# 204 unread single-pass products, in place of twelve unread two-pass ones, in TensorE's first wait of a four-layer trunk

## The chip, the cores and the metric

The kernel runs on one NeuronCore of a Trainium2 chip. The metric is the device time of one execution in microseconds (us); of several runs the median is given. Five engines share the core: TensorE (PE, with its weight loads listed apart as PEld), VectorE (DVE), ScalarE (ACT), GpSimd (POOL) and SyncE (SP, which here only issues transfers). Each runs its own list of instructions in order, and they wait for one another by semaphores.

## The reference

512 rows of 1024 numbers pass through four layers. Each layer normalises the rows, adds a mixer, normalises again and adds a gated feed-forward block. The mixers are, in order, a diagonal state-space mixer (s5), a gated linear attention, a differential attention, and the s5 mixer again. Only the beginning of the first s5 layer matters here. Its core, cut down:

```python
dt = exp(log_dt);  ab_mag = exp(lr * dt);  ab_ang = li * dt
ab_re = ab_mag * cos(ab_ang);  ab_im = ab_mag * sin(ab_ang)
bb = f * b                                   # complex, f from ab and lam
s[t] = ab * s[t-1] + bb @ u[t]               # a scan over the 512 rows
y[t] = real(c @ s[t]) + d_skip * u[t]
z = gelu(y);  a, b = split(z @ w_glu);  x = x + a * sigmoid(b)
```

## The kernel before, in words

Everything is float32. Large products are done as three single-pass products (`mm3`, lines 432 to 434): each operand is split into a high and a low part of type float32r, and high by high, high by low and low by high are summed in one PSUM bank. A single-pass product is one record in the trace. A product of two plain float32 operands, such as a transpose through the identity, takes two passes and leaves two records. Every product has a held operand of 128 rows by up to 128 columns, which a weight load puts into the array, and a streamed operand of up to 512 columns.

`run` calls the layers one after the other, and `s5_first` (line 1594 on) is the first of them. It allocates `zT`, a tile of 128 partitions by 8192 float32r numbers, which the pipeline fills much later (line 1488, from about 56 us on) with the transposed outputs of the mixer. Then it does the following, in the order of the program:

- `s5_small` loads the parameters and turns them with three small transposes (L920, L935). DVE then computes exponentials, sines and powers from them in a long row of small instructions.
- SP queues the loads of `x`, the gains, and the matrices `b` and `c` of the state space (`s5_loads`: `bb` at L1105, `craw` at L1108).
- POOL clears parts of several tiles (`zero_off`, L1176 and L1177).
- `self.hand(PE, Activation)` (line 1639): from here TensorE and ScalarE execute in the order in which the program names the instructions. DVE, POOL and SP are still ordered by the framework's scheduler, until the pipeline calls `hand_all` and writes out the order for all five.
- `s5_qt` (L1141) turns `craw` on TensorE, which needs its transfer. Behind it `warmed(12)` issues twelve products of the identity with itself (L1193) into a bank that nobody reads.
- `s5_in` on ACT squares and scales `x` (L1382, L1383, L1375; POOL takes the root at L523). In between, `rows(0)` turns the phases' rows on TensorE (L1038) and copies them on ACT (L1039).
- DVE copies the turned `craw` into `Q` (L1160) and multiplies it with powers (L1095 to L1097).
- The pipeline `s5_pipe` works through eight groups `kk`. For the first ones, TensorE computes phases (`rough` L1055 and L1056, `angle` L1063 to L1065), turns the input (`up`, L1415) and the operators (`xps`, L1237), and forms the products `V` (L1436). ACT copies and takes sines (L1057, L1059, L1428, L1260, L1071 to L1073), DVE clips (L1068), modulates (L1441 to L1446) and scans (L1450). The map for the direct path goes from TensorE (L1203) over DVE (L1213), ACT (L1217) and two transfers through DRAM (L1219, L1228) to the products `y` (L1470, L1472).

In the feed-forward blocks most products have 256 streamed columns (L575), in the projections 512 (L432 to L434).

Of the kernel before, what the change touches and what calls it, by code (L numbers as in the profile page):

```python
# [11 lines left out]
F32 = mybir.dt.float32  # L12
# [9 lines left out]
P = 128  # L22
# [302 lines left out]
class Trunk:  # L325
# [860 lines left out]
            else:  # L1186
                self.dq.dma_start(d[r, :, g], src[r])

    def warmed(self, n):

        ps = self.sbank("warmed")
        for _ in range(n):
            self.nc.tensor.matmul(ps[:, :P], self.ident[:], self.ident[:], start=True, stop=True)  # L1193

    def s5_rows(self, nb, bp, Q):

# [397 lines left out]
    def s5_first(self, ctx):  # L1594
        nc, i = self.nc, self.i
        xin = self.xp.tile([P, NT, D], F32, tag="x", name="xin")
        zpool = ctx.enter_context(self.tc.tile_pool(name="zT0", bufs=1, side="right"))
        zT = zpool.tile([P, 2, KT, SEQ], F32R, name="zT")
        self.edge(zpool, 32)
        with self.tc.tile_pool(name="s5_0", bufs=1) as p:  # L1600
            scr, more = (self.hp.tile([P, 4096], F32, tag="hT", name=f"scr{z}") for z in range(2))
            oms = [more[:, 1024 * z : 1024 * z + 1024].rearrange("p (a b) -> p a b", a=2) for z in range(2)]
# [33 lines left out]
            with self.tc.issue_after(self.last_power.ins):  # L1636
                new_x(0)
                X[0][2]()
            self.hand(mybir.EngineType.PE, mybir.EngineType.Activation)
            with self.tc.issue_after(self.last_sine.ins):  # L1640
                ps = self.s5_qt(raw[0][1])
                self.warmed(12)
                hu = self.s5_in(scr, xin, (rounded, rows[0]))
            with self.tc.issue_after(self.last_row.ins):
                X[0][3]()
# [6 lines left out]
            room = [four[:, n] for n in range(4)] + [wide[:, 512:], self.np_.tile([P, 512], F32, tag="R", name="z1", bufs=1)[:]]  # L1652
# [851 lines left out]
```

## Time and profile before

| | |
|---|---|
| median of 3 runs | 2279.58 us (2279.41 to 2284.47) |
| span of the profiled execution, first to last instruction | 2272.3 us |
| the profiled execution's own time | not recorded apart from its span; the median lies 7.3 us above it |
| PE busy | 2198.1 us (97%) |
| DVE busy | 1584.4 us (70%) |
| ACT busy | 1109.9 us (49%) |
| POOL busy | 328.0 us (14%) |
| granted TensorE clock, mean | 0.996 |

The span is what the trace shows of one execution; what lies around it (start and end of the program) is in the median alone. A busy share says how long an engine had something to do, not that it set the pace: PE is the bound of most of the span, but in its first 46 us it waits often, and the pace is then set by what it waits for. In rows of the timeline the columns are start (us), length (us), engine, line, operation, output and inputs, shape, count, and in brackets the idle time before and what ended it. Several equal instructions in a row are merged into one line with their count; the length then runs from the first start to the last end.

### The profile page before, as it was taken

How to read it: one execution, taken by the hardware profiler on the slowest of the kernel's cores; microseconds unless marked ns; L12 is line 12 of the kernel's file. 1: busy time of each engine (PE TensorE's matmuls, PEld its weight loads, DVE VectorE, ACT ScalarE, POOL GpSimd, SP SyncE). 2: the span in 40 equal slices, each digit the busy share in tenths (PEclk: the TensorE clock that was granted, in tenths of full speed). 3: DMA queues.
4: the chain of work that ended last, by engine and by line, in shares of the span. 5: the costliest groups of instructions: out<-in, count | busy, mean ns of one | idle time of the engine just before them, and what ended most of it. 6: DMA issues, size and time to landing. Idle time of an engine off the chain costs nothing. (4 is left out here: it accounts for less than half of the span.)

```text
span 2272.3 us, 37257 instructions
## 1 busy us (share of the span) xinstructions
PE 2198.1 (97%) x14871; PEld 1955.4 (86%) x14871; DVE 1584.4 (70%) x2413; ACT 1109.9 (49%) x1779; POOL 328.0 (14%) x446
## 2 busy tenths in 40 slices
PE   6999999999999999999999999999999899999998
PEld 5888889889777799998988887999999888989997
DVE  9965878786525488777745676976766965957675
ACT  6634545454443355554435675644534224635343
POOL 6401142421000010100002231110000000101000
PEclk9999999999999999999999999999999999999999
DMA  4356666663322556665247465985641555766622
GB/s 88 64 171 167 166 157 179 163 180 93 114 76 66 153 154 177 181 172 154 94 139 149 98 148 135 230 213 143 170 100 57 141 155 147 194 172 157 168 75 75
DMA packets 294504, 319.92 MB, mean 141 GB/s; under 512 B 70141, under 2 KB 233241, under 8 KB 294202
## 3 DMA queue, kind: packets, MB, share of 16 engines
q1 hardware_dynamic: 231706, 235.79, 34.1%
q0 software_dynamic: 62624, 81.75, 19.4%
q8 instruction: 117, 1.92, 0.3%
q14 instruction: 57, 0.47, 0.1%
HBM read 285.62 MB, written 16.65 MB: 133 GB/s over the span
## 5 line engine op out<-in xcount | busy, mean ns | idle before, releaser
L412 DVE TENSOR_TENSOR whl<-wst,whl 128x1024 fp32r<-128x1024 f32 x272 | 331.9, 1225 | 267.7 <-ACT whl L404 267.0
L404 ACT CAST whl<-wst 128x1024 fp32r<-128x1024 f32 x272 | 284.5, 1051 | 342.5 <-PE acc L434 242.2
L575 PE MATMUL a<-side,whl 128*128 128x256 f32 x3168 | 383.0, 277 | 6.7 <-DVE whl L412 6.0
L575 PEld LDWEIGHTS a<-side,whl 128*128 128x128 f32 x3168 | 370.2, 188 | 8.9 <-DVE whl L412 6.8
L432 PE MATMUL acc<-whl,act 128*128 128x512 f32 x704 | 278.9, 396 | 1.8 <-DVE g L620 1.6
L433 PE MATMUL acc<-whl,act 128*128 128x512 f32 x704 | 275.7, 392 | 0.0
L434 PE MATMUL acc<-whl,act 128*128 128x512 f32 x704 | 275.7, 392 | 0.0
L575 PE MATMUL c<-side,whl 128*128 128x256 f32 x2112 | 254.8, 277 | 3.6 <-DVE whl L412 3.6
L575 PEld LDWEIGHTS c<-side,whl 128*128 128x128 f32 x2112 | 246.6, 188 | 4.5 <-DVE whl L412 4.4
L412 DVE TENSOR_TENSOR whl<-slot,whl 128x1024 fp32r<-128x1024 f32 x105 | 127.9, 1222 | 64.2 <-ACT whl L404 64.1
L432 PEld LDWEIGHTS acc<-whl,act 128*128 128x128 f32 x704 | 132.6, 188 | 31.7 <-DVE g L620 2.0
L434 PEld LDWEIGHTS acc<-whl,act 128*128 128x128 f32 x704 | 132.5, 188 | 27.9
L433 PEld LDWEIGHTS acc<-whl,act 128*128 128x128 f32 x704 | 132.7, 189 | 26.2 <-issue 0.2
L404 ACT CAST whl<-slot 128x1024 fp32r<-128x1024 f32 x105 | 109.9, 1051 | 74.1 <-PE acc L434 28.2
L432 PE MATMUL acc<-whl,hT 128*128 128x512 f32 x352 | 142.1, 404 | 1.5 <-DVE ro L2233 1.5
L434 PE MATMUL acc<-whl,hT 128*128 128x512 f32 x352 | 137.6, 391 | 0.0
L433 PE MATMUL acc<-whl,hT 128*128 128x512 f32 x352 | 137.4, 390 | 0.0
L575 PE MATMUL d<-sides,whl 128*128 128x256 f32 x1056 | 133.6, 283 | 2.6 <-ACT whl L404 2.6
L575 PEld LDWEIGHTS d<-sides,whl 128*128 128x128 f32 x1056 | 128.9, 191 | 3.4 <-ACT whl L404 3.4
L575 PE MATMUL a<-sides,whl 128*128 128x256 f32 x1056 | 128.9, 278 | 1.7 <-DVE whl L412 1.2
L575 PEld LDWEIGHTS a<-sides,whl 128*128 128x128 f32 x1056 | 124.6, 188 | 3.0 <-DVE whl L412 1.4
L611 POOL DMA_DIRECT2D wst<-in_ffn_w_gate_up_dram x44 | 57.1, 1297 | 442.8 <-DMA wst<-in_ffn_w_gate_up_dram 159.6
(458 smaller groups left out, 3930.0 us busy)
## 6 DMA issues: line engine op xcount, KB each, us to landing
wst<-in_ffn_w_gate_up_dram SPq DMA_DIRECT2D x88, 512.0 KB, 4.4
wst<-in_ffn_w_down_dram SPq DMA_DIRECT2D x88, 512.0 KB, 4.4
slot<-in_ffn_w_gate_up_dram SPq DMA_DIRECT2D x69, 512.0 KB, 6.1
wst<-in_ffn_w_gate_up_dram POOLq DMA_DIRECT2D x44, 512.0 KB, 6.0
halves<-in_ffn_w_gate_up_dram SPq DMA_DIRECT2D x42, 512.0 KB, 5.6
wst<-in_s_w_glu_dram SPq DMA_DIRECT2D x32, 512.0 KB, 4.9
wst<-in_gla_w_in_dram SPq DMA_DIRECT2D x24, 512.0 KB, 3.6
wst<-in_diff_w_qkv_dram SPq DMA_DIRECT2D x24, 512.0 KB, 3.7
```

What stands on the lines that cost most here:

```text
L404: self.last["high"] = self.nc.scalar.copy(hl[:, 0], w[:])
L412: self.last["low"] = self.nc.vector.tensor_tensor(hl[:, 1], w[:], hl[:, 0].bitcast(F32), op=ALU.subtract)
L432: mm(out, lh, rh, start=first, stop=False)
L433: mm(out, lh, rl, start=False, stop=False)
L434: self.last["mm"] = mm(out, ll, rh, start=False, stop=last)
L575: mm(o, hl[:, x, k, c], side[:, y, k], start=first and not (j or k or n), stop=k == 3 and n == 2, skip_group_check=True,)
L611: nc.gpsimd.dma_start(w[:], left.quarter(*plus, b), accum_op=ALU.add)
```

## The change

`warmed` is called ahead of `s5_qt` instead of behind it, and no longer inside the block that orders it behind the last sine. It issues fourteen products of the identity (28 records) where there were twelve (24 records). Behind these come 204 single-pass products on the first 3392 numbers of `zT`, which POOL sets to zero at the start of the layer. They go through four stages: 512 columns forwards (72 products, held rows at 8 offsets), 256 columns forwards (48, at 4 offsets), 512 columns backwards (36, at 4 offsets), 256 columns backwards (48, at 4 offsets). That is 108 products of 512 columns and 96 of 256. All write one PSUM bank, and nothing reads it. The reference's outputs are computed as before.

```diff
-    def warmed(self, n):
+    def warmed(self, room):
 
+        mm = self.nc.tensor.matmul
         ps = self.sbank("warmed")
-        for _ in range(n):
-            self.nc.tensor.matmul(ps[:, :P], self.ident[:], self.ident[:], start=True, stop=True)
+        for _ in range(14):
+            mm(ps[:, :P], self.ident[:], self.ident[:], start=True, stop=True)
+        for back in (False, True):
+            for n, count in ((512, 9), (256, 12)):
+                for at in range(0, 64, 8 if n == 512 and not back else 16):
+                    for j in range(count):
+                        z = (0, 0, 1)[j % 3]
+                        held = room[:, 2048 + 1024 * z + at : 2048 + 1024 * z + at + P]
+                        y = (0, 1, 0)[j % 3]
+                        rows = room[:, 1024 * y : 1024 * y + n]
+                        mm(ps[:, :n], held, rows[:, ::-1] if back else rows, start=j == 0, stop=j == count - 1)
...
         self.edge(zpool, 32)
+        unread = zT[:].rearrange("p z k n -> p (z k n)")
+        nc.gpsimd.memset(unread[:, :3392].bitcast(F32), 0.0)
...
             self.hand(mybir.EngineType.PE, mybir.EngineType.Activation)
+            self.warmed(unread)
             with self.tc.issue_after(self.last_sine.ins):
                 ps = self.s5_qt(raw[0][1])
-                self.warmed(12)
                 hu = self.s5_in(scr, xin, (rounded, rows[0]))
```

## The prediction

> **What bounds the kernel now.** First the page's table of engines, then the timeline of TensorE around the change, the waits, and the engines' shares by stretch.
>
> ```profile
> PE 2198.1 (97%) x14871; PEld 1955.4 (86%) x14871; DVE 1584.4 (70%) x2413; ACT 1109.9 (49%) x1779; POOL 328.0 (14%) x446
> ...
> 5.16 0.30 PE L935 MATMUL s5ps<-ident,params 24*128 24x24 f32 x1 [0.58 <-DVE params L929]
> 15.98 1.12 PE L1141 MATMUL cps<-ident,craw 128*64 128x128 f32 x8 [10.53 <-DMA craw<-in_s_c_re_dram]
> ...
> 23.36 0.60 PE L1038 MATMUL frow<-ident,params 128*12 128x128 f32 x4
> ...
> PE cps L1141 <- DMA craw<-in_s_c_re_dram: 10.5, 1, 10.5
> ...
> 5.50:15.98 10.48, 0.00 (x0) 0.00 (x0) 10.22 (x55) 2.31 (x6) 7.13 (x16) 1.00 0.96 236
> 29.39:46.34 16.95, 12.40 (x142) 10.38 (x142) 16.76 (x26) 15.25 (x26) 9.89 (x13) 0.99 0.44 76
> 46.34:100.00 53.66, 49.24 (x516) 44.00 (x518) 53.36 (x71) 34.37 (x56) 30.65 (x38) 0.97 0.28 59
> ```
>
> TensorE is busy for 2198.1 of 2272.3 us, so over the span it is the bound. The longest gap in it is the one that the change fills: from 5.46 (L935 begins at 5.16 and takes 0.30) to 15.98 it waits for the transfer of craw. The stretch rows (their busy times stand in the order PE, PEld, DVE, ACT, POOL) say who sets the pace afterwards: DVE works for 16.76 of 16.95 us and then for 53.36 of 53.66 us. So in the first layer the pace is DVE's, and TensorE only has to deliver in time. Whatever work of TensorE ends inside those 10.5 us costs nothing; what goes beyond delays the first instruction that DVE or ACT needs from TensorE.
>
> **The change part by part.** First the clearing of zT on POOL.
>
> ```profile
> 0.95 0.20 POOL L347 MEMSET ones<- 128x128 f32 x1
> ...
> 1.45 0.94 POOL L1016 MEMSET frow<- 128x1024 f32 x1
> 4.65 0.24 POOL L991 IOTA params<- 128x128 int32 x1 [2.26 <-PE s5ps L920]
> ...
> 15.75 0.62 POOL L523 TENSOR_TENSOR rs<-ms,mhalf 128x1 f32<-128x1 f32 x1 [2.79 <-issue]
> ```
>
> 128 columns take 0.20 us and 1024 take 0.94, so 3392 take 0.20 + 3264 x 0.74/896 = 2.9 us. It waits for nothing, so it stands where frow's clearing stands, from 1.45 to about 4.35, and pushes that to 5.3. POOL idles for 2.26 us ahead of the iota, so that moves by 0.65 us, and the 2.79 us of idleness ahead of L523 take up the rest. It costs nothing; without this cover it would be 2.9 us at most. TensorE needs the zeros only behind the fourteen identity products, after 10 us.
>
> Then the identity products. Two passes each make 28 records.
>
> ```profile
> 19.08 1.49 PE L1193 MATMUL warmed<-ident 128*128 128x128 f32 x6
> ...
> L1193 PE MATMUL warmed<-ident x24: 274/421/582, 18.5 to 22.9; 128*128 128x128 f32 x24
> ...
> 39.20 1.95 PE L1436 MATMUL V<-room,inm 128*128 128x128 f32 x16
> ```
>
> Of six records the last takes its own 0.421 us, so the steps are (1.49 - 0.421)/5 = 0.214 us. Later the same shape steps at (1.95 - 0.274)/15 = 0.112. TensorE thus begins at half speed, although the granted clock of the windows reads 1.00. 23 steps take 4.4 us (18.5 to 22.9): c slow ones with c x 0.214 + (23 - c) x 0.112 = 4.4 give c = 18, so the speed changes near 22.3 us: 3.8 us after the unbroken work began (18.5) and 6.3 after the first (15.98). I let the slow time last 5.2 us from 5.46 and keep 3.8 and 6.3 as ends. Then 24 records take 5.2 us and four more 0.45: the products begin at 11.1 (10.4 to 11.5). [...]
>
> Then the 204 products.
>
> ```profile
> 301.60 0.40 PE L433 MATMUL acc<-whl,act 128*128 128x512 f32 x1
> ...
> 304.15 0.39 PE L432 MATMUL acc<-whl,act 128*128 128x512 f32 x1
> ...
> 306.64 0.39 PE L434 MATMUL acc<-whl,act 128*128 128x512 f32 x1
> ...
> 333.87 3.02 PE L575 MATMUL d<-sides,whl 128*128 128x256 f32 x24
> 336.73 2.90 PE L575 MATMUL a<-side,whl 128*128 128x256 f32 x24
> 339.47 2.88 PE L575 MATMUL c<-side,whl 128*128 128x256 f32 x24
> 342.19 2.88 PE L575 MATMUL a<-side,whl 128*128 128x256 f32 x24
> ```
>
> From start to start, eleven products of 512 columns take 2.55 us between the first two rows and eleven 2.49 between the second and the third: 0.2318 and 0.2264 each. For 256 columns, 24 take 2.86, 2.74 and 2.72 us: 0.1192, 0.1142 and 0.1133. The same shape thus differs by 2 and 5% with the operands it reads, which is about the spread that offsets may make. I take 0.229 and 0.115: 108 x 0.229 + 96 x 0.115 = 24.7 + 11.0 = 35.7 us, with ends at 35.3 (the lower rows) and 36.5 (the upper). An offset that no row shows could be worse than those; 3% on all of it is 1 us. No row streams backwards. Below, I bound its 36 and 48 products by the same steps; above, by half speed, as the slow records show it for TensorE: 36 x 0.229 + 48 x 0.115 = 13.8 us more. I take the lower, the rows of the same shape, since each column is one read either way. [...]
>
> The products then end at T = 11.1 + 35.7 = 46.8 us. At full speed T could not be below 5.46 + 28 x 0.112 + 35.3 = 43.9.
>
> Next, what is late. TensorE executes in the written order, so s5_qt (ready at 15.98 in the old trace), L1038 (23.36) and all behind them stand behind the products. ACT stops at L1039, which copies L1038's result, and DVE at L1160, which copies s5_qt's.
>
> ```profile
> 42.71 1.09 PE L1141 MATMUL cps<-ident,craw 128*64 128x128 f32 x16
> ...
> 24.29 0.56 ACT L1039 CAST frow<-frow 12x512 fp32r<-12x512 f32 x1
> 24.76 1.15 ACT L1375 ACTIVATE scr<-xin,rs 128x1024 f32<-128x1024 f32 x1
> 28.07 1.17 ACT L1260 COPY inm<-xps 64x512 f32<-64x512 f32 x2 [0.37 <-PE xps L1237]
> ...
> 24.16 0.27 DVE L1160 TENSOR_SCALAR Q<-cps 64x128 f32<-64x128 f32 x1
> 32.95 0.69 DVE L1441 TENSOR_TENSOR mods<-V,cs 128x512 f32<-128x512 f32 x1
> 35.95 1.51 DVE L1446 TENSOR_TENSOR mods<-mods 128x512 f32<-128x512 f32 x1
> 46.48 0.68 DVE L1446 TENSOR_TENSOR mods<-mods 128x512 f32<-128x512 f32 x1
> ```
>
> At full speed s5_qt's sixteen records take 1.09 us. So L1038 starts near T + 0.9 and ends at T + 1.5, where ACT goes on with L1039, which began at 24.29 before: T - 22.8 later. On the way to the first modulation (L1441, 32.95) the 0.37 us of ACT's wait for xps go, because Q is finished sooner: T - 23.2. DVE starts L1160 at T + 0.7 instead of 24.16, T - 23.5. POOL's own row of products for the second half needs nothing of TensorE and is done while TensorE is busy. Today it runs beside DVE, where L1446 takes 1.51 us against 0.68 for the same shape later. So 0.8 us come back, and the pipeline runs T - 24 = 22.8 us late (between T - 23.2 and T - 24.7). Taking away the twelve old products behind s5_qt gives nothing more: they are part of the stretch that is now replaced.
>
> Does a later wait absorb it? It would have to be a wait for something that doesn't hang on the delayed chain.
>
> ```profile
> 46.34 0.77 PE L1470 MATMUL y<-scr,room 128*128 128x128 f32 x2 [2.53 <-DMA scr<-rd]
> ...
> PE a L575 <- DVE whl L412: 1.7, 1, 1.7
> ```
>
> The first transfer that TensorE waits for afterwards is the map (scr from rd), which DVE and ACT write for it, so it shifts with them. The longest wait up to 330 us after that, 1.7 us, is for weights that DVE splits into a buffer freed by TensorE itself. I see no more than 1 us to win back. The sum is **+22.8 us**: the span goes from 2272.3 to 2295.1. The median of before lies 7.3 us above the span, for what the trace doesn't hold, which the change leaves alone: 2279.6 + 22.8 = **2302.4 us**.
>
> **The rivals.**
>
> *Backwards costs twice.* The two backwards stages take 27.6 instead of 13.8 us, and the time is 2316.2. Nothing in the trace shows it or excludes it: 8%.
>
> *The step is the weight load alone.* If a stream of 512 columns could overlap the next one, each product would step like one of 256: 204 x 0.115 = 23.5 us, 12.2 less, 2290.2. Against it stand the rows at 301.60 to 306.64, dense and nowhere below 0.22 us. [...] 3%.
>
> *Not slower: the products leave TensorE in a state in which all pairs step like the best placed.* The place is the body. 1056 records `d<-sides` could gain 0.0059 each, 6.2 us, and at most 4,300 products of 512 columns 0.0054, 23.2 us. It decides from 22.8 of these 29.4 us on; at the full price the time is 2273.0. Against it: the step changes at 304.15 and again at 336.73 without a pause or anything between, so it hangs on the operands at hand and not on history. 2%.
>
> *The change doesn't do what it says.* If products that nobody reads were dropped, or fitted into the wait, the time would stay at 2279.6. They fit only if T is 24 or less, which leaves 12.9 us for 204, 63 ns each, about a quarter to a half of the steps above; and the twelve unread ones are in the trace with all 24 records. 2%.
>
> **How the numbers follow.** The forecast has 80%, backwards 8%, the shorter step 3%, the state 2%, no effect 2%. The other 5% go to a delay that DVE's and POOL's new order changes by more than 3 us, on either side, still slower. The forecast's own ends are T from 45.7 (slow time 3.8, 35.3) to 49 (slow time 6.3, 36.5, 1 us for an unseen offset), and a shift of T - 24.7 to T - 23.2: 21.0 to 25.8 us, 2300.6 to 2305.4. With the spread of the runs of before (2279.4 to 2284.5) and a delay off by 3 us, the range is 2297 to 2310. About 0.3%, 6.8 us, is what a measurement can tell from no change: faster 0.02, same 0.03, slower 0.95.
>
> **What would show it.** In the trace of the changed kernel L1193 should begin near 5.5 us and end near 47. The records step at 0.214 us for 4 to 6 us, then products at 0.226 to 0.232 and 0.113 to 0.120, in all four stages alike. L1141 then comes without a wait, DVE's first L1160 near 47.5, L1441 near 56, and L1470's first near 69. TensorE's busy time rises by about 37 us, and later waits stay. It is wrong if the backwards stages step otherwise, if L1441 follows T by much other than 9 us, or if the body's steps change.

## The result, and the profile after

The changed kernel takes 2300.57 us (median of 3 runs, 2300.42 to 2303.07) against 2279.58: 1.0089 times as long, with a 95% interval of 1.0066 to 1.0111. That is 21.0 us slower; 2302.4 was forecast. In a second set of runs, described below as a repetition, the ratio was 1.0104 [1.0091, 1.0117].

The profiled execution of after took 2300.42 us and has a span of 2298.7, so 1.7 us lie around the span. The page's table of engines, after:

```profile
PE 2234.5 (97%) x15079; PEld 1988.0 (86%) x15079; DVE 1584.1 (69%) x2413; ACT 1110.8 (48%) x1779; POOL 327.7 (14%) x447
```

There are 208 more records on TensorE (204 products, and two identity products of two passes more than the twelve there were), and 36.4 us more busy time. Beside it only the weight loads that belong to these records (PEld) grow, by 32.6 us; the other engines change by less than 1 us. The timeline of TensorE after shows where these 36 us lie. A line number here is ten above that of before from the middle of `warmed` on (twelve in the last part of the file): L1480 is the old L1470, L1446 the old L1436.

```profile
5.08 1.22 PE L1194 MATMUL warmed<-ident 128*128 128x128 f32 x4
...
6.46 3.88 PE L1194 MATMUL warmed<-ident 128*128 128x128 f32 x24
10.10 36.79 PE L1203 MATMUL warmed<-zT 128*128 128x512 f32 x204
46.81 1.09 PE L1141 MATMUL cps<-ident,craw 128*64 128x128 f32 x16
47.84 0.60 PE L1038 MATMUL frow<-ident,params 128*12 128x128 f32 x4
...
69.08 0.46 PE L1480 MATMUL y<-scr,room 128*128 128x128 f32 x2 [1.67 <-DMA scr<-rd]
...
85.61 1.92 PE L1482 MATMUL y<-scr,prods 128*128 128x128 f32 x8
...
99.45 0.50 PE L432 MATMUL acc<-whl,zT 128*128 128x512 f32 x1
```

The wait for craw is gone, and the products fill it and 31 us more: T, at which the next necessary work of TensorE (L1141) begins, is 46.81. The first `y` comes at 69.08 instead of 46.34, 22.7 us late. DVE and ACT show the same delay (timeline of after; in brackets the wait and what ended it):

```profile
47.96 1.21 DVE L1160 TENSOR_SCALAR Q<-cps 64x128 f32<-64x128 f32 x4 [20.79 <-PE cps L1141]
...
56.55 0.69 DVE L1451 TENSOR_TENSOR mods<-V,cs 128x512 f32<-128x512 f32 x1 [2.67 <-ACT cs L1073]
...
59.55 0.68 DVE L1456 TENSOR_TENSOR mods<-mods 128x512 f32<-128x512 f32 x1
```

```profile
48.48 0.57 ACT L1039 CAST frow<-frow 12x512 fp32r<-12x512 f32 x1 [22.91 <-PE frow L1038]
...
54.63 0.62 ACT L1071 ACTIVATE cs<-cs 128x512 f32<-128x512 f32 x1
```

Both engines stand still for over 20 us, DVE until s5_qt's result, ACT until the phases' rows. So the new busy time of TensorE costs what the prediction said it would: not itself, but the part of it that reaches beyond the old wait.

Between the profiled executions the difference is 26.4 us (2298.7 - 2272.3), not 22.7. The rest comes later. The same rows of before, for the second `y` and for the first product behind the pipeline:

```profile
62.57 1.06 PE L1472 MATMUL y<-scr,prods 128*128 128x128 f32 x8
...
74.12 0.50 PE L432 MATMUL acc<-whl,zT 128*128 128x512 f32 x1
```

The eight records take 1.92 us after where they took 1.06 before, and the delay has grown to 25.3 us at L432 (99.45 - 74.12). The busy times by stretch of after (behind the five engines stand the granted clock, the DMA share and GB/s) show what happens there:

```profile
83.50:90.40 6.90, 5.39 (x27) 5.38 (x26) 6.90 (x12) 1.45 (x3) 1.84 (x3) 0.51 0.43 74
...
677.50:680.90 3.40, 3.40 (x10) 2.63 (x9) 0.00 (x0) 0.00 (x0) 0.00 (x0) 0.50 0.22 83
```

TensorE ran at half its clock from 83.6 to 90.4 us, and again for 3.4 us from 677.5, a place where it has no gap at all. In the first of these stretches, where before has the full clock (1.00 from 49.6 to 75; its own half-clock stretch lies at 46.2 to 49.6), the delay grows by 2.5 us, and in the second from 24.4 to 26.0 us; smaller gains and losses in between leave 26.4 at the end. The last section comes back to these stretches, which differ from run to run. Before's profiled execution, at about 2274.0 us if 1.7 us lie around its span too (2272.3 + 1.7), is 5.6 us under its median; the half-clock stretches don't explain that, as the last section shows.

### The profile page after: what moved, and what is told of

Read it like the earlier page. It is cut to its first block, busy times and chain, and to the rows that moved or that the text cites. A ratio compares the mean times of both kernels' runs of the same rounds, so it can differ in the third digit from the quotient of the medians.

```text
span 2298.7 us, 37674 instructions
## 1 busy us (share of the span) xinstructions
PE 2234.5 (97%) x15079; PEld 1988.0 (86%) x15079; DVE 1584.1 (69%) x2413; ACT 1110.8 (48%) x1779; POOL 327.7 (14%) x447
## 5 line engine op out<-in xcount | busy, mean ns | idle before, releaser
L432 PE MATMUL acc<-whl,act 128*128 128x512 f32 x704 | 277.9, 395 | 1.3 <-DVE g L620 1.3
L432 PEld LDWEIGHTS acc<-whl,act 128*128 128x128 f32 x704 | 132.1, 188 | 30.6 <-DVE g L620 1.8
L432 PE MATMUL acc<-whl,hT 128*128 128x512 f32 x352 | 142.7, 405 | 1.1 <-DVE ro L2245 1.1
```

What stands on the lines that cost most here:

```text
L432: mm(out, lh, rh, start=first, stop=False)
```

## The experiments

The theory was that of the prediction: the products cost T - 24, whatever fills TensorE until T, because ACT and DVE wait for what stands behind them (A). The rivals were the other parts of the change: that the identities now come early, that POOL clears 3392 columns, that the scheduler gives DVE another order, and that single placements or directions of the products are dear. The first eight kernels were timed several times beside before (all ratios with their 95% intervals); the last four were profiled once each.

| kernel | T | first y | first y - T | time | ratio |
|---|---|---|---|---|---|
| identities early, nothing else | | 48.51 | | 2280.27 | 1.0007 [0.9998, 1.0016] |
| clearing alone | | 47.68 | | 2279.87 | 1.0006 [0.9998, 1.0015] |
| DVE's order alone | | 51.07 | | 2281.56 | 1.0016 [1.0007, 1.0024] |
| 54 products | 23.95 | 51.33 | 27.4 | 2285.29 | 1.0031 [1.002, 1.0043] |
| 54 products, DVE's old order | 23.20 | 48.67 | 25.5 | 2281.83 | 1.0012 [1.0003, 1.002] |
| 102 products | 29.06 | 53.50 | 24.4 | 2286.79 | 1.0038 [1.0024, 1.0052] |
| the change (204) again | 47.28 | 69.59 | 22.3 | 2302.90 | 1.0104 [1.0091, 1.0117] |
| 408 products | 84.70 | 107.09 | 22.4 | 2340.95 | 1.0276 [1.0261, 1.0292] |
| one sum a stage | 47.06 | 69.30 | 22.2 | 2303.09 | one run |
| sums of double length | 47.22 | 69.50 | 22.3 | 2297.60 | one run |
| eight placements (336 products) | 67.91 | 90.20 | 22.3 | 2322.69 | one run |
| two offsets | 47.52 | 70.11 | 22.6 | 2304.62 | one run |

Before's median beside these runs was 2278.25 (identities early, 54, 102 and 408 products) and 2278.35 (clearing, both kernels on the order, and the repetition); in the single runs 2278.98 for the placements, 2279.39 for the two kernels on sums and 2283.07 for the two offsets.

**Identities early, nothing else.** The 204 products and the clearing are left out of the changed kernel.

```diff
-        for back in (False, True):
-            for n, count in ((512, 9), (256, 12)):
...
-                        mm(ps[:, :n], held, rows[:, ::-1] if back else rows, start=j == 0, stop=j == count - 1)
...
-        nc.gpsimd.memset(unread[:, :3392].bitcast(F32), 0.0)
```

> The changed kernel without the 204 products and without the clearing of zT: the fourteen identity products stay in the first wait. Nothing of the reference's computation is left out. Theory A (the delay is T - 24 us, T being the end of what stands in the wait, and nothing below zero): T is 10.1, so TensorE waits for craw as before, L1038 comes near 23.4 as before, and the time is that of the kernel before within 3 us. Rival C (part of the 21 us comes from the move itself: identity products ahead of s5_qt, the other order of DVE and POOL): this kernel is slower than before by 3 us or more. A point aside: the records of L1141 and behind may run at half speed again, because TensorE idles from 10.1 to 16; by A that costs nothing, since DVE sets the pace.

The interval runs from 0.5 us faster to 3.6 us slower than before. In the profile the pipeline's first `y` begins 2.2 us later (48.51 instead of 46.34). TensorE goes back to half clock in the wait and stays there (stretch of this kernel):

```profile
13.50:30.60 17.10, 8.67 (x62) 6.10 (x63) 16.90 (x72) 13.96 (x25) 8.93 (x14) 0.50 0.33 42
```

In this stretch DVE is the busy engine (16.90 of 17.10 us), so half a clock on TensorE is little felt: DVE's first scan comes 0.7 us later (38.96 instead of 38.26). The rest of the 2.2 us lies in the transfers of the map, for which `y` waits 3.18 us instead of 2.53; why they take longer is not shown. The early identities alone may cost up to 3.6 us, and so are not the cause of the 21.

**54 products.** Of the 204 only the first six offsets of the first stage stay, so that T falls just under the 24 us of theory A.

```diff
-        for back in (False, True):
-            for n, count in ((512, 9), (256, 12)):
-                for at in range(0, 64, 8 if n == 512 and not back else 16):
+        for back in (False,):
+            for n, count in ((512, 9),):
+                for at in range(0, 48, 8):
```

> The changed kernel with only the first 54 products (512 columns forwards, six offsets of nine). Nothing of the reference's computation is left out. At the 0.2333 us that these products take in the changed kernel, T = 10.1 + 54 x 0.2333 = 22.7. Theory A: T - 24 is below zero, so nothing is lost: the time before within 3 us, L1160 of DVE near 24. Rival B (TensorE is the bound, and all that ends behind the old end of the wait is lost): T - 15.98 = 6.7 us slower, 2286. Rival B2 (TensorE's own order sets the delay, from L1038: T - 22.3): 0.4 us slower.

T is 23.95, where 22.7 was planned, still under 24; but the time rises by 0.31%, 7.0 us. Theory A's 0 is refuted at this length. The number of rival B (6.7) fits, but the timeline of DVE shows another cause than a price of the products:

```profile
24.30 0.18 DVE L1033 TENSOR_TENSOR params<-params 128x32 f32<-128x32 f32 x1
...
27.07 1.21 DVE L1160 TENSOR_SCALAR Q<-cps 64x128 f32<-64x128 f32 x4
...
34.69 0.69 DVE L1068 TENSOR_SCALAR cs<-angle 128x512 f32<-128x512 f32 x1
37.35 0.69 DVE L1451 TENSOR_TENSOR mods<-V,cs 128x512 f32<-128x512 f32 x1 [1.97 <-ACT cs L1073]
```

```profile
35.42 0.63 ACT L1071 ACTIVATE cs<-cs 128x512 f32<-128x512 f32 x1 [3.10 <-DVE cs L1068]
```

Two things differ from before. L1033 comes at 24.30 instead of 23.12, in a row of DVE that waits for none of the products. And DVE copies Q (L1160) behind all of its work on X instead of in between (24.16 before), and clips (L1068) behind all of Q, at 34.69 instead of 30.28; ACT waits 3.10 us for that clip, and DVE then 1.97 us for ACT's sines. The next three kernels take these apart.

**The clearing alone**, added to the kernel before, with nothing else.

```diff
+        unread = zT[:].rearrange("p z k n -> p (z k n)")
+        nc.gpsimd.memset(unread[:, :3392].bitcast(F32), 0.0)
```

> The kernel before with nothing but the clearing of zT on POOL added; the twelve products stay where they were. Nothing of the reference's computation is left out. The 54-product run showed three DVE instructions (L915, L996, L1018) taking 1.62, 1.48 and 1.21 us instead of 0.22, 0.35 and 0.15 and all ending when POOL's clearing ends. Theory D (DVE and POOL exclude each other there, so DVE's early row starts 1.2 us later, and DVE sets the pace): L1033 near 24.3 instead of 23.1, the first y near 47.5 instead of 46.3, and the time 1.2 us longer, which the interval of these runs will hardly tell from nothing. Rival, the prediction's claim that the clearing costs nothing: L1033 at 23.1 and the first y at 46.3.

The interval runs from 0.5 us faster to 3.4 us slower, so the time alone decides nothing, but the profile shows the mechanism. Its timeline of POOL and that of DVE:

```profile
1.45 2.91 POOL L1601 MEMSET zT<- 128x3392 f32 x1
...
5.41 0.95 POOL L1016 MEMSET frow<- 128x1024 f32 x1
...
13.86 0.52 POOL L1177 MEMSET scr<- 64x512 f32 x1
```

```profile
2.83 1.62 DVE L915 COPY params<-params 64x128 f32<-64x128 f32 x1 [1.77 <-DMA params<-in_s_log_dt_dram]
2.97 1.48 DVE L996 TENSOR_REDUCE mask<-ident 128x16 f32<-128x128 f32 x1
3.24 1.21 DVE L1018 TENSOR_TENSOR params<-ident 128x4 f32<-128x4 f32 x1
5.18 0.49 DVE L929 COPY params<-s5ps 128x64 f32<-128x64 f32 x3 [0.73 <-PE s5ps L920]
5.59 0.82 DVE L856 TENSOR_SCALAR params<-params 128x64 f32<-128x64 f32 x1
...
13.93 0.50 DVE L944 TENSOR_SCALAR params<-params 128x64 f32<-128x64 f32 x1
...
24.28 0.18 DVE L1033 TENSOR_TENSOR params<-params 128x32 f32<-128x32 f32 x1
```

And before's timeline of DVE:

```profile
2.83 0.22 DVE L915 COPY params<-params 64x128 f32<-64x128 f32 x1 [1.78 <-DMA params<-in_s_log_dt_dram]
2.97 0.35 DVE L996 TENSOR_REDUCE mask<-ident 128x16 f32<-128x128 f32 x1
...
23.12 0.18 DVE L1033 TENSOR_TENSOR params<-params 128x32 f32<-128x32 f32 x1
```

DVE's first three instructions begin when they did, but all of them end at 4.45 us, when POOL's clearing ends (1.45 + 2.91 = 4.36). POOL's instruction takes the 2.9 us that its size let expect. Only half of DVE's loss passes on at once: L929 is 0.57 us late (5.18 instead of 4.61), for DVE waited 1.22 us for TensorE there before and waits 0.73 now. The rest comes later. POOL's other memsets stand later as well, and they now hold up other instructions of DVE: L856 takes 0.82 us instead of 0.20 and ends with the clearing of frow (5.41 + 0.95 = 6.36), and L944 takes 0.50 instead of 0.20 and ends with that of scr (13.86 + 0.52 = 14.38). So L1033 is 1.16 us late, and the first `y` 1.34.

**DVE's order alone**: the kernel before, with the copies of Q held back behind X and the clip behind Q, as in the changed kernel. No products, no clearing.

```diff
-        eng.tensor_tensor(out, out, t[:], op=op)
+        self.last_cross = eng.tensor_tensor(out, out, t[:], op=op)
...
+            with self.tc.issue_after(self.last_cross.ins):
...
+            turned_c = self.last_cross
...
-                phases((0, "clip"), (0, "sines"))
+                with self.tc.issue_after(turned_c.ins):
+                    phases((0, "clip"))
+                phases((0, "sines"))
```

> The kernel before with nothing but DVE's order changed to that of the changed kernel: all of X first, then the four copies L1160, then all of Q, then the clip L1068. No clearing, no products. Nothing of the reference's computation is left out. Theory E (in the 54-product run 3 to 4 us of its 5.0 come from this order, which the scheduler chose because it expected the products to end later; ACT then waits for the clip): the first y comes 2.5 to 4 us later than in the kernel before, 48.8 to 50.3, and the time is longer by as much. Rival F (the order is harmless, and the 5.0 us come from TensorE's own lateness at 24 us): first y at 46.3 and no difference in time.

The time rises by 0.16% (0.07 to 0.24), and DVE's timeline has the pattern of the 54 products:

```profile
25.82 1.20 DVE L1160 TENSOR_SCALAR Q<-cps 64x128 f32<-64x128 f32 x4
...
33.45 0.69 DVE L1068 TENSOR_SCALAR cs<-angle 128x512 f32<-128x512 f32 x1
36.11 0.69 DVE L1441 TENSOR_TENSOR mods<-V,cs 128x512 f32<-128x512 f32 x1 [1.97 <-ACT cs L1073]
```

The wait for ACT's sines is the same 1.97 us, and the first `y` is 4.7 us late, more than the 2.5 to 4 expected.

**54 products in DVE's old order**: the 54 products as above, but the copies of Q come ahead of the end of X, near to the old order.

```diff
             with self.tc.issue_after(self.last_row.ins):
+                Q[0] = self.s5_q(nc.vector, p, 0, 0, 8, 2)
+                Q[0][1](ps, nc.vector)
+            with self.tc.issue_after(self.last_base.ins):
                 X[0][3]()
                 self.s5_b_pads(bp, X[0][0])
-                Q[0] = self.s5_q(nc.vector, p, 0, 0, 8, 2)
-                Q[0][1](ps, nc.vector)
                 Q[0][2]()
-                Q[0][3]()
...
                 phases((0, "clip"), (0, "sines"))
+                Q[0][3]()
```

> The 54-product kernel with DVE's order brought back near that of the kernel before: the copies L1160 ahead of the last third of X, the clip L1068 ahead of the last three instructions for Q. Nothing of the reference's computation is left out. Theory A with D and E (products that end by 24 us cost nothing by themselves): only the clearing's 1.2 us remain, so the first y comes near 47.6 and the time is 1 to 2 us above the kernel before and some 4 us below the 54-product kernel. Rival F: the first y stays at 51.3, the time at 2285.

L1160 is back at 24.87 and the clip at 30.14. The first `y` is 2.3 us late instead of 5.0, and the ratio falls from 1.0031 to 1.0012. So most of what 54 products cost is the order that the scheduler gave DVE once TensorE's program had changed. Of the 2.3 us that are left, 1.3 are those of the clearing alone. The last 1.0 was not expected: DVE's first scan is only 0.3 us behind that of the clearing alone (39.72 against 39.43), but `y` then waits 4.01 us for the map's transfer, where it waited 2.72. Whether the products have a part in that is open.

**102 products**: every second offset of the change.

```diff
-                for at in range(0, 64, 8 if n == 512 and not back else 16):
+                for at in range(0, 64, 16 if n == 512 and not back else 32):
```

> The changed kernel with every second offset of each stage left out: 102 products instead of 204. Nothing of the reference's computation is left out. T = 10.1 + 36.7/2 = 28.5. Theory A: 4.5 us slower than before (2284), or 18 us faster than the changed kernel. Rival B (T - 15.98): 12.5 us slower than before. Rival B2 (T - 22.3): 6.2 us slower. In the profile, the first y (L1480) comes at 46.3 + 4.5 = 50.8 by A.

T is 29.06, and the first `y` is 7.2 us late where A has 5.1 (29.1 - 24). A fails here by 2 us, in the same way as with 54 products, if less: the clip comes behind Q again, and ACT waits 1.88 us for it. Rival B (T - 15.98, here 13.1 us) is refuted: the time rises by 8.7 us, 5.5 to 11.8 by the interval. Rival B2 (T - 22.3) gives 53.1 for the first `y` and is nearer to the 53.50, but it has 48.0 against 51.33 with 54 products, and 108.7 against 107.09 with 408.

**408 products**: the four stages twice.

```diff
-        for back in (False, True):
+        for back in (False, True, False, True):
```

> The changed kernel with all four stages done twice: 408 products. Nothing of the reference's computation is left out. T = 10.1 + 2 x 36.7 = 83.5. Theory A (every further us of products is a us of time): 59.5 us slower than before, 2339, the first y at 105.9. A rival by which later waits for transfers absorb some of the delay, since their data come earlier against the work, gives less than 55. Rival B2 gives 61.2, which the first y in the profile tells from A, though the times alone hardly do.

The stretch of this kernel that holds all the products, and its first `y`:

```profile
11.46:84.70 73.24, 73.24 (x408) 63.40 (x408) 1.00 0.11 13
```

```profile
107.09 0.46 PE L1480 MATMUL y<-scr,room 128*128 128x128 f32 x2 [1.80 <-DMA scr<-rd]
```

Twice the products take 73.24 us, and `y` follows T by 22.4 us, as it does in the change (22.3). The time rises by 62.9 us, within 59.5 to 66.5 by the interval; T - 24 is 60.7. From 204 to 408 products the medians rise by 38 to 40 us for 37.4 to 37.9 more of T. Here A holds.

**The change again**, unaltered, beside the three kernels on DVE's order and the clearing.

> The changed kernel once more, unaltered, with more runs and beside the same runs of the kernel before as the three others. Theory A: first y at T + 22.3, T near 46.8 and a little later if the slow time at the start lasts longer; the time 22 to 25 us above the kernel before. What would speak against it: a difference outside 19 to 28 us, or a first y that does not follow T by 22.3.

2302.90 against 2278.35, a ratio of 1.0104: 23.7 us with an interval of 20.7 to 26.7. T is 47.28 here, since the products began 0.5 us later (10.57), behind a longer slow start.

**Which products are dear.** Four kernels ask why the products took 36.71 us instead of the 35.7 predicted. The stretches of after, one for each stage, holding these products only:

```profile
10.10:26.94 16.84, 16.84 (x73) 13.61 (x73) 1.00 0.55 86
26.94:32.62 5.68, 5.68 (x49) 5.68 (x48) 1.00 0.00 0
32.62:41.02 8.40, 8.40 (x38) 6.78 (x37) 1.00 0.00 0
41.02:46.81 5.79, 5.79 (x49) 5.65 (x47) 1.00 0.01 3
```

(The counts include the neighbours that reach into a stretch.) 72 products of 512 columns forwards step by 0.2339 us, 36 backwards by 0.2333; 48 of 256 by 0.1183 and 0.1206, the last of these with the passage to L1141. Backwards is not dearer than forwards, but the steps are 2 to 5% over the 0.229 and 0.115 taken.

*Eight placements*: sums of 18 and 24 products, forwards only, at eight placements of the held and streamed blocks, the first of them the change's own at offset 0, the others with some or all blocks shifted by 4, 64 or 512 numbers, or with fewer or closer blocks.

```diff
-        for back in (False, True):
...
+        for n, count in ((512, 18), (256, 24)):
+            for helds, streams in place:
```

> The changed kernel with other products in the wait: eight placements of eighteen products of 512 columns, then the same eight with twenty-four products of 256 columns, all forwards, on 4096 cleared numbers. A placement is a pattern of three held and three streamed positions: 0 the pattern of the change (held 2048, 2048, 3072, streamed 0, 1024, 0); 1 held and streamed both fixed; 2 held alternating alone; 3 streamed alternating alone; 4 held 512 numbers further; 5 held 4 numbers further; 6 hi and low parts 64 numbers further apart in both; 7 three held blocks side by side. Nothing of the reference's computation is left out. In the changed kernel all stages step at 0.2333 (512) and 0.1183 us (256), where rows of the body go down to 0.2264 and 0.1133. Theory P (the step hangs on where the held block lies against the streamed one): at least one placement goes to 0.228 or below and 0.115 or below, with the fixed one (1) or those displaced (4, 5, 6) apart from 0. Rival Q (the placement inside one tile does not matter; the difference to the body has another source): all eight within 0.002 of 0.2333 and within 0.002 of 0.1183.

Neither theory's picture came out: after some ten products the 512-column step settled at 0.2267 us and stayed there through all the other placements; the 256-column step was 0.120, but 0.1184 where the held blocks lay 4 numbers further.

*One sum a stage*: the first and last product of a stage alone begin and end a sum.

```diff
-                        mm(ps[:, :n], held, rows[:, ::-1] if back else rows, start=j == 0, stop=j == count - 1)
+                        mm(ps[:, :n], held, rows[:, ::-1] if back else rows, start=at + j == 0, stop=at >= last and j == count - 1)
```

> The changed kernel, but each of the four stages is one sum in its bank (one first product that starts it, one last that ends it) instead of 8, 4, 4 and 4 sums of nine or twelve. Same 204 products, same operands, same order. Theory G: the ends of the sums cost something, and the steps of 0.2333 (512 columns) and 0.1183 us (256) are 0.2267 plus 0.06 us for each end; then the steps here fall to 0.2267 and 0.113, T falls from 46.8 to about 46.1. Theory H: the step is set by the phase in which the sequence of products began, and the ends of sums cost nothing; then the steps stay at 0.233 and 0.118 and T at 46.8 (within 0.3, for the end of the slow start moves).

The four stages take 16.84, 5.69, 8.40 and 5.78 us, as before. Ends of sums cost nothing: G is refuted.

*Sums of double length*, at half as many offsets (0, 16, 32, 48 forwards; 0 and 32 in the other stages).

```diff
-            for n, count in ((512, 9), (256, 12)):
-                for at in range(0, 64, 8 if n == 512 and not back else 16):
+            for n, count in ((512, 18), (256, 24)):
+                for at in range(0, 64, 16 if n == 512 and not back else 32):
```

> The changed kernel, but with sums of 18 and 24 products at half as many offsets (4, 2, 2 and 2) instead of nine and twelve at 8, 4, 4 and 4. Still 204 products in the same four stages. Theory G (each end of a sum costs 0.06 us): steps near 0.230 and 0.116, T near 46.4. Theory H (phase alone): 0.233 and 0.118 and T near 46.8, or another fixed step from some product on that isn't the first of a sum.

T is 47.22, and the steps of the first 18 products settle at 0.2267 and change to 0.231 and 0.235 with the 19th, where the offset becomes 16. That product is also the first of a sum; the last kernel parts the two.

*Two offsets*: 0 in the first half of each stage, 16 in the second, with sums of nine and twelve as in the change.

```diff
-                        held = room[:, 2048 + 1024 * z + at : 2048 + 1024 * z + at + P]
+                        shift = 16 * (at // 32)
+                        held = room[:, 2048 + 1024 * z + shift : 2048 + 1024 * z + shift + P]
```

> The changed kernel, but the held rows have only two offsets: 0 in the first half of each stage's products and 16 numbers in the second half (the change has 8 and 4 offsets from 0 to 56). All else is the same. Theory O: the offset sets the step; then the 512-column steps forwards settle at 0.2267 us within the first nine or so and go to about 0.2333 at the 37th product, where the offset becomes 16, and backwards at the 19th; T near 46.5. Theory H: the offset does nothing and the step is that of the sequence's own phase; then no change shows at the 37th and the 19th product, and T is 46.1 to 47.

Its stretches, each half stage by itself:

```profile
10.99:19.25 8.26, 8.25 (x36) 6.85 (x37) 1.00 0.82 101
19.25:27.65 8.40, 8.40 (x37) 6.77 (x36) 1.00 0.16 20
27.65:30.52 2.87, 2.87 (x25) 2.87 (x24) 1.00 0.00 0
30.52:33.35 2.83, 2.83 (x26) 2.83 (x25) 1.00 0.00 0
33.35:37.56 4.21, 4.21 (x21) 3.39 (x19) 1.00 0.00 0
37.56:41.76 4.20, 4.20 (x20) 3.38 (x18) 1.00 0.00 0
```

The first 36 products take 8.26 us, 0.2267 each behind a first one of 0.31; from the 37th on it is 8.40, 0.2333 each, and the starts in the trace show the step change at that very product. For 256 columns it goes the other way, 0.1197 at offset 0 and 0.1179 at 16. Backwards both halves step by 0.2333. So O is right forwards: of these two offsets of the held rows, each has its step, 3% apart. Backwards, where O had a change at the 19th product, it fails. For 512 columns, backwards costs nothing beside the change's other offsets and 3% beside the best one.

## Why the prediction was right, and where not

- **The bound, and that the products cost only what reaches beyond the wait**: right. ACT and DVE stop at L1039 and L1160, as said, the first modulation came at 56.55 where the prediction had it near 56, and the first `y` at 69.08 where it had it near 69.
- **Products dropped, or hidden in the wait**: refuted; all 204 are in the trace, and T is 46.81.
- **Slow start** (5.2 us, products from 11.1): mis-sized. The step goes from 0.213 to 0.111 us 3.4 us after 5.08, and the products began at 10.10; in the other kernels they began between 10.35 and 12.06. The start varies with the run.
- **204 products, 35.7 us**: mis-sized, 36.71. The prediction put all rows at 0.229 and 0.115 and kept 1 us, 3%, for an offset that no row shows; the step at the change's offsets (0.233) took just that. The products' early start and their longer steps, two errors of 1 us, cancelled in T (46.8 and 46.81): that T came out to the hundredth is luck.
- **Backwards costs twice**: refuted by the third stage, 0.2333 us a step. The lower of the two bounds had been chosen by an argument alone (one read a column either way), which no row of before showed; the runs show the step. **The weight load alone**: refuted by every 512-column step, none of which settled under 0.2267. **A state that speeds up the body**: refuted. The costliest group of the page takes, before and after:

```profile
L575 PE MATMUL a<-side,whl 128*128 128x256 f32 x3168 | 383.0, 277 | 6.7 <-DVE whl L412 6.0
```

```profile
L575 PE MATMUL a<-side,whl 128*128 128x256 f32 x3168 | 383.5, 277 | 7.0 <-DVE whl L412 6.0
```

- **Clearing hidden behind POOL's idle time**: the length was right (2.91 us for 2.9), the step was wrong. The prediction looked at what POOL delays on its own queue, and the price is on DVE, 1.2 us: half from the clearing itself, half from the small memsets that it pushes back. It is hidden all the same, by DVE's wait of 20.79 us for Q, so that it enters the change's time with nothing; with 54 products it is on the path.
- **Delay T - 24**: right where T is long, from 46.8 to 84.7, where `y` follows T by 22.2 to 22.6 us in every kernel. Below that `y` - T is larger than the 22.3 that T - 24 stands for: 25.5 and 27.4 at 54 products and 24.4 at 102. The rival of no effect, where the products "fit only if T is 24 or less", had the wrong point: at T = 23.95 the time still rises by 7.0 us. The 0.8 us of L1446 did come back (L1456 takes 0.68 us after). Where T is long, POOL's products are done by then, and DVE has finished X whatever the order (it stands idle for the 20.79 us). The clip behind Q then holds nobody up: ACT goes from L1059 to L1071 (54.63) without a wait.
- **Nothing later absorbs the delay**: right, and nothing did. But half-clock stretches move, which the prediction didn't have. In after the one at 83.6 adds 2.5 us and the one at 677.5 1.6, while before loses as much in one of its own at 285 us and has it back by 292, where after's TensorE waits 1.89 us for DVE and its own waits 0.34.
- **7.3 us between span and median, "for what the trace doesn't hold"**: wrong. Only 1.7 us lie around the span; the other 5.6 are that before's profiled execution was a quick one (the quickest of 29 later runs of before took 2274.22). Since a median was added to a difference of spans, the error didn't reach the forecast.

## What to carry to other kernels

Work that is put into an engine's wait and reaches far beyond it costs what reaches beyond the time at which other engines need its results. That time can be read from one profile: here the first `y` was forecast within 0.2 us, helped by two errors that cancelled. But a reordered program also changes the order in which a scheduler serves the other engines, and when the work just fits, that order is the price, here 5 us of first output where the sum said none. A memset on POOL is not free because POOL is idle (the one of 2.91 us here made DVE's L1033 1.16 us late): look at what DVE does in the same microseconds, and beside the memsets that are pushed back. And before a span is compared with a median, see from a second execution how far spans vary.

## What the runs showed of the hardware

**Half-clock stretches come in a fixed length, at places that depend on the run.** By the granted clock in the traces of before and after all of them, but that at the end of the program (6.09 and 5.34 us), last 3.41 us or twice that; the 17.1 us of the kernel with the identities early are five such lengths. They start at 46.16, 285.09, 1769.89 and 1776.71 us in before and at 83.55, 677.47, 1793.63 and 1803.87 in after. Within each of the two traces these starts lie whole multiples of 3.413 us apart (in after 593.92 us from 83.55 to 677.47, 174 lengths; in before 238.93 us from 46.16 to 285.09, 70 lengths), as on one grid. The timeline of after shows what stands ahead of the one at 677.5: no gap, but 32 products of two columns.

```profile
672.65 3.63 PE L1975 MATMUL dps<-ind,la 128*128 128x2 f32 x32
...
677.72 0.63 PE L432 MATMUL acc<-whl,hT 128*128 128x512 f32 x1
```

The row of L432 takes 0.63 us there, and 0.39 elsewhere. The repetition of the same kernel, and beside it the kernel with sums of double length, in the same stretch:

```profile
675.00:681.90 6.90, 6.90 (x24) 6.00 (x24) 0.36 (x1) 0.20 (x1) 0.00 (x0) 0.51 0.27 76
```

```profile
675.00:681.90 6.90, 6.90 (x41) 6.04 (x41) 0.94 (x1) 0.20 (x1) 0.00 (x0) 1.00 0.25 76
```

The repetition has two such lengths, the other kernel none: 24 records against 41 in the same 6.9 us. Why one run has such a length at a place and another has none, no run here shows.

Among executions of the same 204 products the time goes with these stretches. With T taken off the span and the one at the end of the program left out, the five executions of 204 products give 2248.7 us (3 lengths of 3.41 us, mean granted clock 0.997; sums of double length), 2251.9 (5, 0.996; after), 2252.4 (5, 0.996; the repetition), 2254.2 (7, 0.994; one sum a stage) and 2255.4 (8, 0.994; two offsets): 1.3 us for each on average, where half a clock for 3.41 us could by arithmetic cost up to 1.7. Over all kernels they are not enough. From the first `y` to the end, before's execution took 2226.0 us with four lengths (mean granted clock 0.996), the one with the clearing alone 2229.8 with three (0.997), and the one with 408 products 2232.0 with three (0.997). Between 657 and 1769 us of before, where its clock is full, the kernel with the clearing falls back against before from 2.9 to 5.5 us, in part at a wait for ACT of 1.54 us near 1500 that before doesn't have. So executions also differ by microseconds for another reason, which stays open, and with it the 5.6 us by which before's profiled execution was quick.

**POOL's memset holds some instructions of DVE up until it ends.** With the clearing alone, a copy, a reduction and a tensor_tensor on DVE took 1.62, 1.48 and 1.21 us instead of 0.22, 0.35 and 0.15, and all ended with the memset (4.45 us, POOL's at 4.36). Not all are held: in after a tensor_tensor with two inputs in SBUF (L1021, 128x512, at 9.21) ran beside two memsets of POOL (9.13 to 9.43 and 9.47 to 9.78) and took 0.69 us; the same shape takes 0.68 with POOL idle (L1456, at 59.55). So a memset doesn't hold every tensor_tensor, and the one among the three may only have stood behind the other two. What sets the held ones apart no run here shows.

**A product's step depends on where its held rows begin.** 512 columns step by 0.2267 us at offset 0 and 0.2333 at offset 16 (64 bytes), 256 columns by 0.1197 and 0.1179. Shifts by 4, 64 and 512 numbers left the 0.2267 as it was; for 256 columns that by 4 brought 0.1184 in place of 0.120. Why a shift by 16 matters for 512 columns and those do not, why the two widths go opposite ways, and why backwards has 0.2333 at both offsets stays open.
